# 32x32 transposes in the last step of the modulation, and 128-row operands in the attention scores of two layers

## The chip, the cores and the metric

The kernel runs on one core of a Trainium2 chip. The metric is the device time of one execution in microseconds (us); less is better. The engines of the core have names of their own in the profile: PE is TensorE (matrix products; PEld its loading of weights), DVE VectorE, ACT ScalarE, POOL GpSimd, and SP the queue that issues most of the DMAs.

## The reference, cut to what matters

Two layers over 512 latent tokens and 256 context tokens of width 1024. Each layer takes six vectors (shift, scale and gate for each of two sub-layers) from a conditioning vector, for the latent tokens from `c` and for the context tokens from `c_ctx`. Layer 0 mixes tokens by a recurrence and by windowed attention with a sink, layer 1 by latent attention (`_mla_latent`) and a convolution; each ends in a mixture of experts.

```python
def _modulation(cond, w, b):
    m = (jax.nn.silu(cond) @ w + b)[..., None, :]
    return jnp.split(m, 6, axis=-1)

# layer 0, windowed heads (width 64)
s_win = jnp.einsum('bnqkgd,bnmkd->bnkgqm', qb, kb).astype(jnp.float32) * scale
s_ctx = jnp.einsum('bnqkgd,bckd->bnkgqc', qb, k_ctx).astype(jnp.float32) * scale
s_sink = _sink_column(sink, kvh, g, s_win.shape[:-1] + (1,))
p = jax.nn.softmax(jnp.concatenate([s_win, s_ctx, s_sink], axis=-1), axis=-1)

# layer 1, heads of width 64 + 32
s = jnp.einsum('bqhd,bkhd->bhqk', q, k).astype(jnp.float32) * q.shape[-1] ** -0.5
p = jax.nn.softmax(s, axis=-1).astype(v.dtype)

def reference(...):
    for layer in range(DEPTH):
        m_l = _modulation(c, w_mod[layer], b_mod[layer])
        m_c = _modulation(c_ctx, w_mod[layer], b_mod[layer])
        h_l = _modulate(x_lat, m_l[0], m_l[1])
        ...
        x_lat = _layer_norm(DN_ALPHA * x_lat + m_l[2] * y_l, ...)
        f_l = _modulate(x_lat, m_l[3], m_l[4])
        ffn = _hier_moe(tokens, ...)
        x_lat = _layer_norm(DN_ALPHA * x_lat + m_l[5] * ffn, ...)
```

## The kernel before

Tokens lie along the free axis: 512 latent ones, 4 of padding, 256 of context, W = 772 columns in all. All weights come through one ring of 2 MB buffers that SP fills in the order of their use (`Stream`); a buffer is handed back with `K.stream.done`. The program is written as a sequence of stages (the mixer of layer 0, its routing and experts, the mixer of layer 1, its routing and experts, the output); inside them the order of the instructions on each engine is set by the scheduler of the tile framework, which runs a model of the timeline while it builds (`schedule_with_timeline_sim=True`, line 2273). Each engine then runs its own list in order, and an instruction that waits holds what stands behind it on that engine.

**Modulation.** One section (one of the six vectors of a layer, 1024 wide, for `c` and `c_ctx` together) is computed by `modulation(K, l, sec)` in two halves of 512. `modulation_rows` (line 213) streams a half of the weights through PE as `qmod`: eight products of 32 columns by 512, two to each group of 32 partitions (line 219), so that the four partial sums of a row stand in partitions 0, 32, 64 and 96 for `c` and one below for `c_ctx`. ACT copies `qmod` from PSUM into `msb` (line 222). What is still to be done is to add the four partial sums and to turn the row into columns, since the vectors are used along the partitions. That is `finish()`: 16 products, each with 64 strided columns of `msb` as weights and a 128x2 constant `pick` as the moving operand (line 239), into `fmp`, and one addition on DVE that writes `fm` (line 240). The mixers call this as filling between their own steps: `fill()` runs the `finish()` of the section before and then starts the next. Sections 0 and 1 of layer 0 are done in the beginning by other lines (L364). The other ten go through `modulation`: sections 2 to 5 of layer 0 and sections 0 and 1 of layer 1 in the mixer of layer 0 (line 499), sections 2 to 5 of layer 1 in the attention of layer 1 (line 1987).

**Scores of layer 0.** `maxima(t)` forms a bound of the scores of four heads, as four rows of high and low parts, and turns them by PE into `mT`, a tile of 4 partitions by 768 (lines 583 to 587). `scores` (line 614) adds that bound to the scores inside PSUM by a third product, with `sel`, four rows of a 0/1 constant, as weights and `mT` as moving operand (line 627 for the context's own queries, line 637 for the others). `normalise` uses the same four rows for the sink (line 693).

**Scores of layer 1.** `operands(h, w)` (line 1901) writes, for each head, the high and low parts of queries and keys (`qh`, `ql`, `kh`, `kl`), 96 partitions of values; two more partitions of `kh` hold ones and of `qh` the negative maximum. `mx` (lines 1935 and 1940) are the products for that maximum, `scores` (line 1996) the three products of a block of 128 keys (lines 1999 to 2001), the last of them over 98 partitions. Even heads take their tiles from one pool, odd ones from another, one of each kind.

Of the kernel before, what the change touches and what calls it, by code (L numbers as in the profile page):

```python
# [11 lines left out]
F = mybir.dt.float32  # L12
# [22 lines left out]
def host_arrays(inp):  # L35
# [6 lines left out]
    a["xT"] = x.reshape(NT, 8, 128).transpose(2, 1, 0)  # L42
    a["wmod"] = i["w_mod"].reshape(2, 128, 8, 12, 512).transpose(0, 3, 1, 2, 4).reshape(2, 12, 128, 4096)
    a["lng"], a["lnb"] = i["ln_g"], i["ln_b"]
# [71 lines left out]
    cf["pick"][0::32, 0] = cf["pick"][1::32, 1] = 1  # L116
    cf["eps"] = np.full((128, 1), EPS)
    F_off, o = {}, 0
    for k, v in cf.items():
# [92 lines left out]

def modulation_rows(K, s):

    nc = K.nc
    q = K.ps.tile([128, 512], F, tag="b", name="qmod")
    for k in range(2):
        for c in range(4):
            nc.tensor.matmul(q[32 * c:32 * c + 32], K.cond[:, 2 * c + k, :],  # L219
                             s[0][:, 1024 * c + 512 * k:1024 * c + 512 * k + 512], start=(k == 0), stop=(k == 1))  # L220
    m = K.mp.tile([128, 512], F, tag="msb", name="msb", bufs=2)
    nc.scalar.activation(m, q, AF.Copy)
    return m


def modulation(K, l, sec):

    nc = K.nc
    ms = []
    for b in range(2):  # L230
        s = K.stream.get(("mod", l, sec, b))
        ms.append(modulation_rows(K, s))
        K.stream.done(s)

    def finish():
        t = K.ps.tile([128, 512], F, tag="b", name="fmp")
        for b in range(2):
            for j in range(8):
                nc.tensor.matmul(t[64 * b:64 * b + 64, 2 * j:2 * j + 2], ms[b][:, j::8], K.cst["pick"], start=True, stop=True)
        nc.vector.tensor_tensor(K.fm[:, l, :, sec], t[:, 0:16].rearrange("p (j i) -> p i j", j=8),  # L240
                                K.fmb[:, l, None, sec].to_broadcast([128, 2, 8]), op=ALU.add)

    return finish
# [47 lines left out]
def mixer_even(K):  # L291
# [260 lines left out]
    def maxima(t):  # L552
# [31 lines left out]
        for b in range(6):  # L584
            PE.transpose(q[0:4, 128 * b:128 * b + 128], nb[:, b, :], c["identb"])
        mT = up.tile([4, 768], BF, tag="mT", name="mT", bufs=2)
        V.tensor_copy(mT, q[0:4, 0:768])
        early.append((qs, mT))
# [25 lines left out]
    def scores(h, qs, mT, unit_):  # L614
# [4 lines left out]
        p = ap.tile([128, 512], F, tag="P", name="P", bufs=9)  # L619
        sel = c["sel"][0:4, 128 * par:128 * par + 128]  # L620
        if kind == "x":
# [63 lines left out]
    def normalise(t, mT, ol, oc, sums):  # L685
# [3 lines left out]
        for o, s, n, r0, m0 in ((ol, 0, 512, 0, 0), (oc, 1, 256, C0, 512)):  # L689
            dn, es = ps("dn"), ps("es")  # L690
            for i in range(2):
                PE.matmul(dn[64 * i:64 * i + 64, 0:n], c["onesf"][:, 0:64], sums[i][s][:, 0:n], start=True, stop=True)
            PE.matmul(es[:, 0:n], c["sel"][0:4, 256:384], mT[:, m0:m0 + n], start=True, stop=True)
            e = ap.tile([128, 512], F, tag="es", name="es", bufs=2)
            S.activation(e[:, 0:n], es[:, 0:n], AF.Exp, scale=0.125, bias=sk)
            V.tensor_add(e[:, 0:n], e[:, 0:n], dn[:, 0:n])
            V.reciprocal(e[:, 0:n], e[:, 0:n])
            V.tensor_mul(att[:, r0:r0 + n], o[:, 0:n], e[:, 0:n])
# [969 lines left out]
def mixer_odd(K, uh, hh, hl):  # L1668
# [232 lines left out]
    def operands(h, w):  # L1901
# [11 lines left out]
        V.tensor_add(f[64:96], f[64:96], r[64:96])  # L1913
        pool = ap if h % 2 else op
        qh = pool.tile([98, NL], FR, tag="qh", name="qh")
        ql = pool.tile([96, NL], FR, tag="ql", name="ql")
        S.activation(qh[0:96], f, AF.Copy)
        V.tensor_sub(ql, f, qh[0:96].bitcast(F))
        if h < 2:
            khs[h] = pool.tile([98, W], FR, name="kh%d" % h)  # L1920
        kh = khs[h % 2]
        kl = pool.tile([96, W], FR, tag="kl", name="kl")
        for q, (s0, s1) in zip(kq, both):
# [9 lines left out]
        for b in range(4):  # L1933
            q = ps("mx")
            PE.matmul(q, qh[0:96, 128 * b:128 * b + 128], kh[0:96, 0:NL], start=True, stop=True)
            V.tensor_reduce(mx[:, b, 0:1], q, axis=AX.X, op=ALU.max)
        for b in range(0, 4, 2):
            q = ps("mx")
            for i in range(2):
                PE.matmul(q[:, 256 * i:256 * i + 256], qh[0:96, 128 * (b + i):128 * (b + i) + 128], kh[0:96, C0:W],  # L1940
                          start=True, stop=True)
# [54 lines left out]
    def scores(kh, kl, qh, ql):  # L1996
        for n, tk in enumerate(toks):
            q = ps("s")
            PE.matmul(q, kh[0:96, tk:tk + 128], ql, start=True, stop=False)
            PE.matmul(q, kl[:, tk:tk + 128], qh[0:96], start=False, stop=False)  # L2000
            PE.matmul(q, kh[:, tk:tk + 128], qh, start=False, stop=True)
# [204 lines left out]
def setup(ctx, tc, a, pvo, cfo, cbo):  # L2206
# [20 lines left out]
    def prologue(K):  # L2227
# [8 lines left out]
        K.cst = dict(ident=f("ident"), onesf=f("ones"), iota=f("iota"), iota2=f("iota2"), down=f("down"), tokc=f("tokc"),  # L2236
                     zero=f("zero"), pick=f("pick"), eps=f("eps"), tri=g("tri"), ones=g("ones"), identb=g("ident"), mge=g("mge"),
                     mle=g("mle"), sel=g("sel"))
# [40 lines left out]
```

## Time and profile before

| | us |
|---|---|
| median of 3 runs | 2051.74 |
| lowest, highest | 2051.34, 2056.99 |
| the profiled execution | 2062.3 |
| its span in the trace | 2060.5 |
| PE busy | 1810.0 (88% of the span) |
| PE weight loads | 950.9 (46%) |
| DVE busy | 911.9 (44%) |
| ACT busy | 471.7 (23%) |
| POOL busy | 481.9 (23%) |

The profile is one execution, with times in us from the start of its span. Busy times of PE are lengths of records that overlap, so that the distance between the starts of two neighbours tells better what one costs. A line in it is a line of the kernel before; the changed kernel has its lines 5 to 18 further down. The "granted clock" of PE is given as a share of its upper level, 2.4 GHz; 0.5 is its lower level, 1.2 GHz, and a stretch in between holds both.

### The profile page before, as it was taken

The page shows a single profiled execution, that of the slowest core. Times are in us where ns is not written, and L with a number is a line of the kernel's source. Part 1 is how long each engine was busy: PE and PEld are TensorE (multiplying, and loading weights), DVE is VectorE, ACT ScalarE, POOL GpSimd, SP SyncE. Part 2 cuts the span into 40 slices and gives each one's busy share as a digit, 9 for nine tenths or more (in the row PEclk, how much of TensorE's full clock was granted, in tenths as well). Part 3 has the DMA queues.
Part 4 walks back from the last instruction along what each step waited for, and adds up shares of the span by engine and source line. Part 5 has one row for each costly group of instructions (what it writes and reads, how often), then busy time and mean ns, then how long its engine had stood idle before and what let it go on. Part 6 is the DMA issues. An engine that isn't in the chain of part 4 may idle for free. (4 is left out here: it accounts for less than half of the span.)

```text
span 2060.5 us, 23254 instructions
## 1 busy us (share of the span) xinstructions
PE 1810.0 (88%) x8514; PEld 950.9 (46%) x8515; DVE 911.9 (44%) x1631; ACT 471.7 (23%) x794; POOL 481.9 (23%) x415
## 2 busy tenths in 40 slices
PE   5999999995998989999967787999769999998785
PEld 3668644684333333333335663556633333333232
DVE  3676531577221221222167888465833233322127
ACT  3472322322010110101035453334310000000001
POOL 2142335333000000100033656334100010000103
PEclk9989898996999999999988797889879999999997
DMA  8741320426698999998982112424559999999973
GB/s 350 274 156 42 123 85 1 164 102 256 264 426 371 411 425 424 408 395 349 373 334 92 41 42 110 175 83 187 225 214 423 427 404 400 424 424 425 424 311 150
DMA packets 59023, 551.87 MB, mean 268 GB/s; under 512 B 13295, under 2 KB 13807, under 8 KB 28018
## 3 DMA queue, kind: packets, MB, share of 16 engines
q1 hardware_dynamic: 43490, 514.47, 61.1%
q0 software_dynamic: 11056, 21.00, 2.7%
q10 hardware_dynamic: 4320, 14.31, 1.8%
q8 instruction: 98, 1.61, 0.3%
q14 instruction: 59, 0.48, 0.1%
HBM read 535.00 MB, written 33.61 MB: 276 GB/s over the span
## 5 line engine op out<-in xcount | busy, mean ns | idle before, releaser
L916 PE MATMUL q<-ring,xT 128*64 128x512 f32 x1024 | 475.6, 608 | 43.5 <-PEq L1148 27.9
L917 PE MATMUL q<-ring,xT 128*64 128x512 f32 x1024 | 476.6, 609 | 5.6 <-DMA ring<-in_w_dram 5.6
L945 PE MATMUL q<-ring,hT 128*64 128x512 f32 x1152 | 297.6, 605 | 24.8 <-DMA ring<-in_w_dram 10.9
L916 PEld LDWEIGHTS q<-ring,xT 128*64 128x64 f32 x1024 | 132.3, 139 | 296.4 <-issue 264.6
L925 ACT ACTIVATE sl<-q 64x512 f32<-64x512 f32 x72 | 42.6, 592 | 752.1 <-PE q L917 742.4
L878 POOL DMA_INDIRECT xg<-f,tok x38 | 39.1, 1029 | 591.3 <-DVE tok L873 402.9
L945 PEld LDWEIGHTS q<-ring,hT 128*64 128x64 f32 x1152 | 88.7, 138 | 180.5 <-issue 167.4
L917 PEld LDWEIGHTS q<-ring,xT 128*64 128x64 f32 x1024 | 132.9, 139 | 28.5 <-issue 18.7
L935 DVE COPY hT<-q 128x256 f32<-128x256 f32 x72 | 30.6, 425 | 232.2 <-PE q L933 231.8
L263 PE MATMUL pj<-hh,wlo 128*128 128x512 f32 (+2 forms) x336 | 107.3, 371 | 12.9 <-DVE wlo L252 12.9
L263 PE MATMUL pj<-hl,whi 128*128 128x512 f32 (+2 forms) x336 | 105.0, 364 | 0.0
L263 PE MATMUL pj<-hh,whi 128*128 128x512 f32 (+2 forms) x336 | 104.6, 365 | 0.0
L1815 POOL TENSOR_TENSOR acc<-acc,prod 128x512 f32<-128x512 f32 x56 | 86.5, 1545 | 54.9 <-ACT prod L1814 52.0
L851 DVE TENSOR_TENSOR oh<-cf,pos 128x512 fp32r<-128x512 f32 (+1 forms) x65 | 53.3, 823 | 98.8 <-PE qi L865 97.8
L953 DVE TENSOR_TENSOR y<-q,m 64x512 f32<-64x512 f32 x70 | 48.2, 689 | 83.3 <-PE q L945 75.1
L891 DVE COPY xT<-qx 128x512 f32<-128x512 f32 x32 | 22.1, 692 | 123.2 <-PE qx L887 123.2
L956 DVE COPY y<-q 64x512 f32<-64x512 f32 x37 | 25.7, 693 | 113.9 <-ACT y L955 75.8
L926 DVE SCALAR_TENSOR_TENSOR h<-q,gate,sl 64x512 f32<-64x512 f32 x68 | 51.0, 749 | 56.4 <-ACT sl L925 35.4
L263 PEld LDWEIGHTS pj<-hh,wlo 128*128 128x128 f32 (+1 forms) x336 | 58.4, 195 | 28.9 <-DVE wlo L252 15.1
L1810 DVE SCALAR_TENSOR_TENSOR acc<-glu,pv,acc 128x512 f32<-128x512 f32 x60 | 70.9, 1187 | 0.9
L219 PE MATMUL qmod<-ring,cond 128*32 128x512 f32 x384 | 61.9, 786 | 10.6 <-ACT cond L2241 10.6
L916 PE MATMUL q<-ring,xTo 128*64 128x512 f32 x128 | 61.7, 639 | 8.0 <-DVE xTo L900 8.0
(523 smaller groups left out, 3144.1 us busy)
## 6 DMA issues: line engine op xcount, KB each, us to landing
ring<-in_w_dram SPq DMA_DIRECT2D x192, 2048.0 KB, 18.7
ring<-in_wmod_dram SPq DMA_DIRECT2D x24, 2048.0 KB, 8.7
ring<-Y SPq DMA_DIRECT2D x8, 1024.0 KB, 9.3
ring<-in_ew_dram SPq DMA_DIRECT2D x3, 2048.0 KB, 14.9
f<-t ACTq DMA_DIRECT2D x10, 512.0 KB, 3.3
xhat<-xh ACTq DMA_DIRECT2D x9, 512.0 KB, 3.7
ring<-in_ewo_dram SPq DMA_DIRECT2D x2, 2048.0 KB, 10.1
ring<-in_ow_dram SPq DMA_DIRECT2D x2, 2048.0 KB, 10.2
```

The costliest lines, as they stand in the source:

```text
L219: nc.tensor.matmul(q[32 * c:32 * c + 32], K.cond[:, 2 * c + k, :], s[0][:, 1024 * c + 512 * k:1024 * c + 512 * k + 512], start=(k == 0), s ...
L263: nc.tensor.matmul(q[0:m, 0:s1 - s0], a[:, k, 0:m], b[k][:, s0:s1], start=(k == i == 0), stop=(k == 7 and i == 2))
L851: V.tensor_tensor(oh.rearrange("p t (n s) -> p t n s", n=n), iota[:, None, None, :].to_broadcast([128, T, n, 64]), pos[:, :, e:e + n, None ...
L878: return G.indirect_dma_start(out=x[0:m], out_offset=None, in_=K.f, in_offset=bass.IndirectOffsetOnAxis(ap=tok[0:m], axis=0), bounds_check ...
L916: PE.matmul(q[a:a + 64], xT[:, k, :], w1[:, 512 * k:512 * k + 512], start=(k == 0), stop=(k == 7))
L917: last = PE.matmul(q[b:b + 64], xT[:, k, :], w3[:, 512 * k:512 * k + 512], start=(k == 0), stop=(k == 7)).ins
L925: S.activation(sl[a:a + 64], q[a:a + 64], AF.Silu)
L926: V.scalar_tensor_tensor(h[a:a + 64], q[b:b + 64], gate[a:a + 64], sl[a:a + 64], op0=ALU.mult, op1=ALU.mult)
L945: K.last_mm = PE.matmul(q[64 * o:64 * o + 64], hT[:, k, :], w2[:, 1024 * k + 512 * o:1024 * k + 512 * o + 512], start=(k == 0), stop=(k == ...
L953: V.tensor_mul(y[:, b], q[a], K.m5[a, b])
L1810: V.scalar_tensor_tensor(y, g[:, k:k + NL], w(k), y, op0=ALU.mult, op1=ALU.add)
L1815: G.tensor_add(z, z, p)
```

## The change

It has three parts.

1. `modulation()` no longer copies `qmod` on ACT. DVE transposes it, 32x32 block by 32x32 block, out of PSUM into `msb` (two of 128x512 for each of the ten sections, 20 in all). The weights are laid out on the host in another order of columns, so that each block holds 32 neighbouring elements of the vector. `finish()` then needs 8 products in place of 16, each with a 128x32 constant (`stack`, four unit matrices one below the other) as weights and 8 columns of `msb` as moving operand. The four older sums at line 364 stay as they are.
2. In layer 0 `mT` gets 128 partitions, 124 of them zeroed by POOL, and `sel` is used with all its 128 rows, whose other rows are zero: 64 products in `scores` and 8 in `normalise`.
3. In layer 1 `kh`, `kl`, `qh` and `ql` are tiles of 128 partitions, allocated once for even and once for odd heads; POOL zeroes partitions 96 to 127 of each, and from the third head on it zeroes the two rows of `qh` that held the maximum before. `mx` and `scores` use all 128 partitions.

The diff:

```diff
--- before.py
+++ after.py
@@ -40,7 +40,11 @@
     x = np.concatenate([i["x"][0], i["ctx"][0]], 0)
     a["x"] = x
     a["xT"] = x.reshape(NT, 8, 128).transpose(2, 1, 0)
-    a["wmod"] = i["w_mod"].reshape(2, 128, 8, 12, 512).transpose(0, 3, 1, 2, 4).reshape(2, 12, 128, 4096)
+    wm = i["w_mod"].reshape(2, 128, 8, 12, 512).transpose(0, 3, 1, 2, 4)
+
+    wp = i["w_mod"].reshape(2, 128, 8, 6, 4, 32, 2, 4).transpose(0, 3, 6, 1, 2, 4, 7, 5).reshape(2, 12, 128, 8, 512)
+    first = (np.arange(24).reshape(2, 12) < 4)[:, :, None, None, None]
+    a["wmod"] = np.where(first, wm, wp).reshape(2, 12, 128, 4096)
     a["lng"], a["lnb"] = i["ln_g"], i["ln_b"]
     ew = i["e_w_in"][0].reshape(8, 128, 1792).transpose(1, 0, 2)
     cols = np.concatenate([np.arange(512, 1024), np.arange(1536, 1792), np.arange(1024, 1536), np.arange(0, 512)])
@@ -115,6 +119,7 @@
     cf["pick"] = np.zeros((128, 2))
     cf["pick"][0::32, 0] = cf["pick"][1::32, 1] = 1
     cf["eps"] = np.full((128, 1), EPS)
+    cf["stack"] = np.tile(np.eye(32), (4, 1))
     F_off, o = {}, 0
     for k, v in cf.items():
         F_off[k] = (o, v.shape[1])
@@ -210,7 +215,7 @@
     return K.pv[:, o:o + w]
 
 
-def modulation_rows(K, s):
+def modulation_parts(K, s):
 
     nc = K.nc
     q = K.ps.tile([128, 512], F, tag="b", name="qmod")
@@ -218,8 +223,13 @@
         for c in range(4):
             nc.tensor.matmul(q[32 * c:32 * c + 32], K.cond[:, 2 * c + k, :],
                              s[0][:, 1024 * c + 512 * k:1024 * c + 512 * k + 512], start=(k == 0), stop=(k == 1))
+    return q
+
+
+def modulation_rows(K, s):
+    q = modulation_parts(K, s)
     m = K.mp.tile([128, 512], F, tag="msb", name="msb", bufs=2)
-    nc.scalar.activation(m, q, AF.Copy)
+    K.nc.scalar.activation(m, q, AF.Copy)
     return m
 
 
@@ -229,14 +239,19 @@
     ms = []
     for b in range(2):
         s = K.stream.get(("mod", l, sec, b))
-        ms.append(modulation_rows(K, s))
+        q = modulation_parts(K, s)
         K.stream.done(s)
+
+        m = K.mp.tile([128, 512], F, tag="msb", name="msb", bufs=2)
+        nc.vector.transpose(m, q)
+        ms.append(m.rearrange("p (n y) -> p n y", y=32))
 
     def finish():
         t = K.ps.tile([128, 512], F, tag="b", name="fmp")
         for b in range(2):
-            for j in range(8):
-                nc.tensor.matmul(t[64 * b:64 * b + 64, 2 * j:2 * j + 2], ms[b][:, j::8], K.cst["pick"], start=True, stop=True)
+            for g in range(4):
+                nc.tensor.matmul(t[32 * g:32 * g + 32, 8 * b:8 * b + 8], K.cst["stack"], ms[b][:, 4 * g:4 * g + 4, 0:2],
+                                 start=True, stop=True)
         nc.vector.tensor_tensor(K.fm[:, l, :, sec], t[:, 0:16].rearrange("p (j i) -> p i j", j=8),
                                 K.fmb[:, l, None, sec].to_broadcast([128, 2, 8]), op=ALU.add)
 
@@ -583,8 +598,9 @@
         q = K.ps.tile([128, 1024], BF, tag="b", name="mT")
         for b in range(6):
             PE.transpose(q[0:4, 128 * b:128 * b + 128], nb[:, b, :], c["identb"])
-        mT = up.tile([4, 768], BF, tag="mT", name="mT", bufs=2)
-        V.tensor_copy(mT, q[0:4, 0:768])
+        mT = up.tile([128, 768], BF, tag="mT", name="mT", bufs=2)
+        G.memset(mT, 0.0)
+        V.tensor_copy(mT[0:4], q[0:4, 0:768])
         early.append((qs, mT))
 
     mix, early = [], []
@@ -617,7 +633,7 @@
         q = ps("st")
         kind, j = unit_
         p = ap.tile([128, 512], F, tag="P", name="P", bufs=9)
-        sel = c["sel"][0:4, 128 * par:128 * par + 128]
+        sel = c["sel"][:, 128 * par:128 * par + 128]
         if kind == "x":
             for j in range(2):
                 o = q[:, 256 * j:256 * j + 256]
@@ -690,7 +706,7 @@
             dn, es = ps("dn"), ps("es")
             for i in range(2):
                 PE.matmul(dn[64 * i:64 * i + 64, 0:n], c["onesf"][:, 0:64], sums[i][s][:, 0:n], start=True, stop=True)
-            PE.matmul(es[:, 0:n], c["sel"][0:4, 256:384], mT[:, m0:m0 + n], start=True, stop=True)
+            PE.matmul(es[:, 0:n], c["sel"][:, 256:384], mT[:, m0:m0 + n], start=True, stop=True)
             e = ap.tile([128, 512], F, tag="es", name="es", bufs=2)
             S.activation(e[:, 0:n], es[:, 0:n], AF.Exp, scale=0.125, bias=sk)
             V.tensor_add(e[:, 0:n], e[:, 0:n], dn[:, 0:n])
@@ -1911,15 +1927,17 @@
         V.tensor_mul(f[64:96], qn[64:96], rope[64:96, 0])
         V.tensor_mul(r[64:96], qn[96:128], rope[96:128, 1])
         V.tensor_add(f[64:96], f[64:96], r[64:96])
-        pool = ap if h % 2 else op
-        qh = pool.tile([98, NL], FR, tag="qh", name="qh")
-        ql = pool.tile([96, NL], FR, tag="ql", name="ql")
+        if h < 2:
+
+            pool = ap if h else op
+            khs[h] = [pool.tile([128, n], FR, name="%s%d" % (nm, h)) for nm, n in (("kh", W), ("kl", W), ("qh", NL), ("ql", NL))]
+            for x in khs[h]:
+                G.memset(x[96:128].bitcast(F), 0.0)
+        kh, kl, qh, ql = khs[h % 2]
+        if h > 1:
+            G.memset(qh[96:98].bitcast(F), 0.0)
         S.activation(qh[0:96], f, AF.Copy)
-        V.tensor_sub(ql, f, qh[0:96].bitcast(F))
-        if h < 2:
-            khs[h] = pool.tile([98, W], FR, name="kh%d" % h)
-        kh = khs[h % 2]
-        kl = pool.tile([96, W], FR, tag="kl", name="kl")
+        V.tensor_sub(ql[0:96], f, qh[0:96].bitcast(F))
         for q, (s0, s1) in zip(kq, both):
             src = q[0:64, 0:s1 - s0]
             S.activation(kh[0:64, s0:s1], src, AF.Copy)
@@ -1932,12 +1950,12 @@
         mx = op.tile([128, 4, 2], F, tag="mx", name="mx", bufs=2)
         for b in range(4):
             q = ps("mx")
-            PE.matmul(q, qh[0:96, 128 * b:128 * b + 128], kh[0:96, 0:NL], start=True, stop=True)
+            PE.matmul(q, qh[:, 128 * b:128 * b + 128], kh[:, 0:NL], start=True, stop=True)
             V.tensor_reduce(mx[:, b, 0:1], q, axis=AX.X, op=ALU.max)
         for b in range(0, 4, 2):
             q = ps("mx")
             for i in range(2):
-                PE.matmul(q[:, 256 * i:256 * i + 256], qh[0:96, 128 * (b + i):128 * (b + i) + 128], kh[0:96, C0:W],
+                PE.matmul(q[:, 256 * i:256 * i + 256], qh[:, 128 * (b + i):128 * (b + i) + 128], kh[:, C0:W],
                           start=True, stop=True)
             V.tensor_reduce(mx[:, b:b + 2, 1], q.rearrange("p (i n) -> p i n", i=2), axis=AX.X, op=ALU.max)
         V.tensor_tensor(mx[:, :, 0:1], mx[:, :, 0:1], mx[:, :, 1:2], op=ALU.max)
@@ -1996,8 +2014,8 @@
     def scores(kh, kl, qh, ql):
         for n, tk in enumerate(toks):
             q = ps("s")
-            PE.matmul(q, kh[0:96, tk:tk + 128], ql, start=True, stop=False)
-            PE.matmul(q, kl[:, tk:tk + 128], qh[0:96], start=False, stop=False)
+            PE.matmul(q, kh[:, tk:tk + 128], ql, start=True, stop=False)
+            PE.matmul(q, kl[:, tk:tk + 128], qh, start=False, stop=False)
             PE.matmul(q, kh[:, tk:tk + 128], qh, start=False, stop=True)
             p = ap.tile([128, NL], F, tag="P", name="P", bufs=NP)
             S.activation(p, q, AF.Exp, scale=scale)
```

What the scheduler makes of it: the order of the big steps stays, and the lists differ by the operations that come and go. On PE, in layer 0 behind the third chunk of the projection (`chunk(2)`, `pj`), the rows before are (`fmp` is the finish of a section, `qmod` the products of the next, `gate` the recurrence):

```order
L263 MATMUL pj<-hh,whi 128x512
L263 MATMUL pj<-hh,whi 128x260
L239 MATMUL fmp<-cf,msb 64x2 x16
L219 MATMUL qmod<-ring,cond 32x512 x16
L437 MATMUL gate<-uc,ring 128x512
```

and after:

```order
L278 MATMUL pj<-hh,whi 128x512
L278 MATMUL pj<-hh,whi 128x260
L253 MATMUL fmp<-msb,cf 32x8 x8
L224 MATMUL qmod<-ring,cond 32x512 x16
L452 MATMUL gate<-uc,ring 128x512
```

Sixteen narrow products have become eight, and nothing else has moved. On DVE, at the first `fill()` in layer 0, beside the convolution of the recurrence (`uc`) and the split of the projection's weights (`wlo`), the rows before are:

```order
L421 TENSOR_SCALAR uc<-u,pv 128x772
L423 SCALAR_TENSOR_TENSOR uc<-u,pv,uc 128x772
L252 TENSOR_TENSOR wlo<-ring,whi 128x1024
L423 SCALAR_TENSOR_TENSOR uc<-u,pv,uc 128x772
L252 TENSOR_TENSOR wlo<-ring,whi 128x1024
L421 TENSOR_SCALAR uc<-u,pv 128x772
L423 SCALAR_TENSOR_TENSOR uc<-u,pv,uc 128x772 x4
```

and after:

```order
L436 TENSOR_SCALAR uc<-u,pv 128x772
L246 STREAM_TRANSPOSE msb<-qmod 128x512
L438 SCALAR_TENSOR_TENSOR uc<-u,pv,uc 128x772
L267 TENSOR_TENSOR wlo<-ring,whi 128x1024 x2
L438 SCALAR_TENSOR_TENSOR uc<-u,pv,uc 128x772
L246 STREAM_TRANSPOSE msb<-qmod 128x512
L436 TENSOR_SCALAR uc<-u,pv 128x772
L438 SCALAR_TENSOR_TENSOR uc<-u,pv,uc 128x772 x4
```

The two transposes stand in DVE's list where ACT had its copies before; the first of them, which waits for `qmod`, now stands ahead of the first `wlo`.

## Rows read from the trace of the kernel before

**Rows 1.** Windows by stage: stretch, length, busy us (count) per engine, clock, DMA.

```profile
46.00:230.00 184.00, 181.81 (x1081) 139.96 (x1079) 124.18 (x145) 91.13 (x133) 58.12 (x60) 0.96 0.39 147
230.00:385.00 155.00, 153.20 (x632) 73.60 (x625) 52.06 (x71) 50.19 (x93) 70.25 (x76) 0.87 0.21 82
1230.00:1271.00 41.00, 25.38 (x105) 12.91 (x104) 40.52 (x48) 19.88 (x40) 31.13 (x21) 0.79 0.26 103
1271.00:1420.00 149.00, 142.29 (x703) 85.53 (x703) 84.06 (x138) 53.52 (x101) 51.41 (x43) 0.85 0.27 103
```

**Rows 2.** The sum of the same windows for the tile fmp alone.

```profile
sum 529.00, PE 35.52 PEld 34.78 DVE 1.74; mean PE 8.88 PEld 8.69 DVE 0.43
```

**Rows 3.** Timeline of PE, two finishes: start, length, engine, line, operation, tiles, shapes.

```profile
308.81 3.55 PE L239 MATMUL fmp<-cf,msb 128*64 128x2 f32 x32
...
1275.71 3.55 PE L239 MATMUL fmp<-cf,msb 128*64 128x2 f32 x32
```

**Rows 4.** Windows around finishes; the clock is the third number from the end.

```profile
121.00:128.00 7.00, 7.00 (x41) 2.29 (x40) 4.66 (x6) 6.24 (x9) 3.87 (x10) 0.51 0.04 4
271.00:275.00 4.00, 4.00 (x24) 1.25 (x26) 0.18 (x1) 0.00 (x0) 0.70 (x1) 0.57 0.00 0
309.00:312.00 3.00, 3.00 (x31) 3.00 (x31) 0.00 (x0) 0.52 (x2) 3.00 (x3) 1.00 0.00 0
312.00:333.00 21.00, 21.00 (x50) 8.46 (x49) 0.18 (x1) 3.54 (x7) 8.63 (x16) 0.51 0.00 1
1278.00:1285.00 7.00, 7.00 (x39) 2.56 (x42) 1.25 (x5) 0.60 (x1) 2.20 (x3) 0.52 0.21 43
1329.00:1333.00 4.00, 4.00 (x23) 1.27 (x27) 0.61 (x4) 0.14 (x1) 1.27 (x6) 0.57 0.02 4
```

**Rows 5.** Timeline of PE in layer 1, the nearest narrow products.

```profile
1401.25 1.09 PE L2025 MATMUL rs<-rT,cf 8*64 8x128 f32 x16
```

**Rows 6.** Timeline of PE in layer 0 around a product with sel.

```profile
231.72 0.28 PE L636 MATMUL st<-qs,k 128*128 128x256 f32 x1
231.93 0.28 PE L637 MATMUL st<-mT,cb 4*128 4x256 bf16 x1
232.14 0.23 PE L642 MATMUL st<-cb 128*128 128x128 bf16 x1
...
232.38 0.28 PE L570 MATMUL mw<-k,qs 128*128 128x256 f32 x1
232.50 0.23 PE L574 MATMUL mw<-cb 128*128 128x128 bf16 x1
```

**Rows 7.** Timeline of PE in layer 1, products over 128 and over 96 partitions.

```profile
1258.16 0.40 PE L1895 MATMUL qn<-cqn,wh 128*128 128x512 f32 x1
1258.40 0.40 PE L1896 MATMUL qn<-cqn,wh 128*128 128x512 f32 x1
...
1260.38 0.40 PE L1999 MATMUL s<-ql,kh 96*128 96x512 f32 x1
1260.62 0.40 PE L2000 MATMUL s<-qh,kl 96*128 96x512 f32 x1
```

**Rows 8.** Page, costliest groups: DVE reading a 128x512 tile out of PSUM.

```profile
L891 DVE COPY xT<-qx 128x512 f32<-128x512 f32 x32 | 22.1, 692 | 123.2 <-PE qx L887 123.2
```

**Rows 9.** Tile qmod: who waited for it (us, times), over the whole run.

```profile
  ACT msb L222: 67.9, 19
```

**Rows 10.** Timeline of the first fill in layer 0, with idle time and releaser in brackets.

```profile
59.39 3.63 PE L219 MATMUL qmod<-ring,cond 128*32 128x512 f32 x30
...
60.56 1.02 DVE L423 SCALAR_TENSOR_TENSOR uc<-u,pv,uc 128x772 f32<-128x772 f32 x1
...
61.50 1.22 DVE L252 TENSOR_TENSOR wlo<-ring,whi 128x1024 fp32r<-128x1024 f32 x1
...
62.95 0.30 PEld L263 LDWEIGHTS pj<-hh,wlo 128*128 128x128 f32 x2 [0.84 <-DVE wlo L252]
```

**Rows 11.** POOL's zeroing of two rows in layer 1, by line.

```profile
L1928 POOL MEMSET kh<- x2: 737/858/978, 1198.6 to 1226.9; 2x772 f32 x2
```

More of the change, by code (lines that the diff above doesn't have):

```diff
@@ L2236, in prologue @@
         K.cst = dict(ident=f("ident"), onesf=f("ones"), iota=f("iota"), iota2=f("iota2"), down=f("down"), tokc=f("tokc"),
-                     zero=f("zero"), pick=f("pick"), eps=f("eps"), tri=g("tri"), ones=g("ones"), identb=g("ident"), mge=g("mge"),
+                     zero=f("zero"), pick=f("pick"), eps=f("eps"), stack=f("stack"), tri=g("tri"), ones=g("ones"), identb=g("ident"), mge=g("mge"),
                      mle=g("mle"), sel=g("sel"))
```

## The prediction

> **What bounds the kernel now.** I read the windows by stage first, because the share of busy time on the page is a mean over stages with different limits. The change acts in three of them. In the mixer of layer 0 PE is busy 181.81 of 184 us and 153.20 of 155, in the attention of layer 1 behind 1271 us 142.29 of 149; DVE, ACT and POOL have room there (DVE 124, 52 and 84 us) [rows 1]. What PE saves in these stretches is time. Between 1230 and 1271 it is the other way round: DVE is busy 40.52 of 41 us and PE 25.38, so there a DVE instruction more is time. The transfers don't hold these stages up: their share is 0.21 to 0.39 [rows 1].
>
> The last column but two of the same rows is the second reading: the granted clock is 0.96, 0.87 and 0.85. A stretch of length t at clock c has lost t x (1 - c), at most, against full clock: 184 x 0.04 + 155 x 0.13 + 149 x 0.15 = 7 + 20 + 22 = 50 us. Third, I asked for the tile `fmp`, what runs where the clock falls, and for the neighbours of the products that change.
>
> **Part 1, the finish.** The ten finishes take 35.52 us of PE [rows 2], 3.55 us each in 32 records (16 products, two records each), 111 ns a record [rows 3]. PE does nothing else in that time. The new finish has 8 products, thus 16 records, over a 32-column weight with 8 moving columns. The trace has no such form. Its nearest row is 16 records of 64-column weights with 128 moving columns in 1.09 us, 68 ns each [rows 5]. From below I take half of that, 0.55 us, since the columns of both operands are fewer; from above the old price of a record, 16 x 0.111 = 1.78 us. I take 1.09, the row, as the neighbour in size and count. The saving is 10 x (3.55 - 1.09) = 24.6 us, between 10 x (3.55 - 1.78) = 17.7 and 10 x (3.55 - 0.55) = 30. All of it lies in PE-bound stretches.
>
> The Trainium skill, "TensorE: Matmul & The Clock Gate", section "LDWEIGHTS (loading the stationary operand)", says that loading weights takes as long as their columns divided by 1.2 GHz, whatever the rows. By it 32 columns take 27 ns, and if the load alone set the pace, 160 records would take 4.3 us and the saving would be 31 us; but by it 64 columns would take 53 ns, and the old finish shows 111 [rows 3].
>
> **Part 2, `sel` with 128 rows.** Between products over 128 partitions of 256 columns the starts lie 0.12 us apart (232.38 to 232.50); into the product over 4 partitions they lie 0.21 apart (231.72 to 231.93), and out of it 0.21 again (231.93 to 232.14) [rows 6]. So a change of the number of rows costs about 0.09 us each way. Of the 64 products in `scores`, 48 are followed by another over 128 partitions and 128 columns, and save 0.18; 16 are followed by products with 64-column weights, which stay another form, and save 0.09: 48 x 0.18 + 16 x 0.09 = 10.1 us. The 8 in `normalise` I leave out. The bounds are 0, if the extra belongs to the bf16 product and not to its rows, and 72 x 0.18 = 13. POOL's four zeroings of `mT` have no reader near: POOL is busy 70 of 155 us there [rows 1], and `mT` is needed a whole pair of heads later; if one were late, it would cost what the nearest row of zeroing takes, 0.86 us each [rows 11].
>
> **Part 3, 96 rows to 128 in layer 1.** Products over 96 partitions follow each other at 0.24 us (1260.38 to 1260.62), those over 128 at 0.24 too (1258.16 to 1258.40) [rows 7]. Nothing is gained or lost on PE. The zeroings on POOL (four for each of the first two heads, one for each later head) cost at most 8 x 0.86 + 6 x 0.86 = 12 us of POOL, by the row of a zeroing that is as long and has fewer rows [rows 11]. POOL is busy 31 of 41 and 51 of 149 us [rows 1], so I take 0 and keep, for the first head of each pool, two late ones in the range: 2 us.
>
> **Part 4, the transposes on DVE.** ACT loses 20 copies, DVE gains 20 transposes. No transpose is in the trace; the nearest row is DVE's copy of a 128x512 tile out of PSUM, 0.69 us [rows 8]. 20 x 0.69 = 13.8 us of DVE is the bound from above by load, 0 that from below. Most of it falls where DVE has room. Two places are different. At the first fill in layer 0 the first transpose now stands ahead of the first `wlo`, and PE waits for `wlo` already (0.84 us at 62.95). `qmod` runs from 59.39 for 3.63 us in two halves, so that its first half is there at 61.2; the transpose ends at 61.9, the `uc` that started at 60.56 ends 1.02 later, 62.9, and `wlo` 1.22 later, at 64.1, against 62.72 before [rows 10]: 1.4 us. And in the DVE-bound stretch from 1230 to 1271 two transposes (the section started there) cost 1.4 us, and up to 1 us of waiting for `qmod`: 2.4. Together 4 us.
>
> **Part 5, the clock.** The clock is 1.00 during the finish at 308.81, and from 312 to 333 it is 0.51, though PE is busy without a gap [rows 4]. Five of the falls come with the end of a finish, this one, that at 1275.71 [rows 3] and three others: 121 to 128 (0.51), 271 to 275 (0.57), 312 to 333, 1278 to 1285 (0.52) and 1329 to 1333 (0.57) [rows 4]. In each PE had been at two-column products for some 3 us. They cost 7 x 0.49 + 4 x 0.43 + 21 x 0.49 + 7 x 0.48 + 4 x 0.43 = 3.4 + 1.7 + 10.3 + 3.4 + 1.7 = 20.5 us. With the finish down to about 1 us in a stream of wide products I expect all five to go, and of the other 29 us (50 - 20.5), which fall at stalls and at rows of narrow products elsewhere, a small part, 4 us, since fewer drains keep PE fuller; but new falls may come elsewhere. I take 24.5 us; the bounds are 0 and 50.
>
> **The sum.** 24.6 + 10.1 + 24.5 - 4 = 55 us off the profiled 2062.3, that is 2007. That execution took 10.6 us more than the median of the runs; the same difference from 2051.74 is 1997 us. All terms at their poorest (17.7 + 0 + 0, less 13.8 of DVE and 2 of POOL) give 2050, all at their best (30 + 13 + 50 - 0) 1959; that they all fall on one side I hold for unlikely.
>
> **Rivals.** *The clock doesn't come back.* The falls may belong to something else in the same places (the `qmod` products with 32-column weights come directly behind each finish and stay). For it: not every fall follows a finish, as half of the 50 us shows. Against it: five of ten finishes have one at their end, and the clock is full while they run (309 to 312) [rows 4]. Then the gain is 24.6 + 10.1 - 4 = 31, and the time 2021.
>
> *The rows of `sel` give nothing*, since a product over few rows takes as long as one over 128 and the extra comes from its type. Then 45 us remain: 2007. Against it: the product behind it, which is bf16 too, is late as well, while the bf16 product at 232.50 isn't [rows 6]. The Trainium skill, "TensorE: Matmul & The Clock Gate", section "Why this matters for your kernels", has this rule for a single product over 32 rows; rows 7 agree for 96, rows 6 don't for 4.
>
> *The gain of layer 0 is given back.* If the experts of layer 0 wait for weights, an earlier end of the mixer gains only what the stream of weights moves up too. Of the 55 us some 37 lie in layer 0 (6 of 10 finishes 15, `sel` 10, clock 15, less 3). Against it: the share of the transfers is 0.21 in this stage [rows 1], so the stream stands waiting for buffers that the mixer hands back, and moves with it. Then 18 us remain: 2034.
>
> *Slower.* DVE's list is in order, and a transpose that waits for `qmod` holds what stands behind it. ACT sat 67.9 us in its waits for `qmod`, 19 times over 24 copies [rows 9]; 20 of these on DVE would be 56.6 us, with the transposes' own 13.8 it is 70 us. If all of it reached PE and the clock did not come back, the sum would be 70 - 35 = +35: 2087. It decides from the point where 35 us of it, half, reach PE. Against it: where PE is the bound, DVE idles by 103 and 65 us [rows 1], and a wait for the bound engine's own product is idle time that DVE had anyway.
>
> **How the numbers follow.** Forecast (a gain of 40 us and more, the clock back for most of it) 0.60; clock not back 0.20; `sel` nothing 0.07; given back 0.05; slower 0.06; no difference 0.02. A measurement of this kernel can tell 0.3%, 6 us. Faster by more: 0.60 + 0.20 + 0.07 + 0.05 = 0.92; within 0.02; slower 0.06. The range takes in the first three cases and the bounds of the clock as far as they are likely: from 2051.74 - 82 = 1970 to 2051.74 - 19 = 2033.
>
> **What would show it.** In the profile after, the tile `fmp` should take 11 us of PE in place of 35.5. Neighbours of the products with `sel` should stand 0.12 us apart at 256 columns. The granted clock from 312 to 333 us should be 1.00, and the stages' clocks 0.92 and more. No idle time of PE put down to `msb` or `wlo` should exceed 2 us at the first fill. The forecast is wrong if the stretches behind the finishes stay at 0.5, if PE waits for DVE between 46 and 385 us, or if the experts start earlier and end no earlier.

## The result and the profile after

The changed kernel takes 1994.94 us (median of 4 runs, 1992.5 to 2011.23), the kernel before 2054.36 beside it: a ratio of 0.972 with an interval of 0.9669 to 0.977, so 57 us less (47 to 68; every "us less" below is worked out from such a ratio in the same way). Run once more on another chip (below) it gave 0.9702 (0.9678 to 0.9726). The forecast was 1997, the range 1970 to 2033.

The execution that left the trace took 2011.23 us, the longest of the four; where that lies is told at the end. The stretches that a reader should compare are not equal times but equal work: from the first finish to the sixth, from there to the experts of layer 0, and from the seventh finish to the tenth (the finishes are counted in the order in which they run: six in layer 0, four in layer 1). Windows of the kernel before (columns as in [rows 1]):

```profile
71.55:308.81 237.26, 233.28 (x1265) 157.56 (x1264) 137.35 (x175) 105.48 (x158) 80.27 (x72) 0.93 0.32 123
308.81:509.46 200.65, 177.97 (x806) 120.53 (x805) 111.21 (x212) 55.02 (x94) 86.52 (x71) 0.85 0.32 122
1275.71:1357.21 81.50, 77.72 (x423) 43.79 (x422) 41.24 (x77) 25.12 (x53) 28.17 (x27) 0.85 0.39 155
```

and of the changed kernel:

```profile
71.41:281.51 210.10, 200.07 (x1180) 137.59 (x1183) 145.84 (x185) 100.19 (x149) 82.76 (x74) 0.98 0.35 137
281.51:467.22 185.71, 162.88 (x790) 116.65 (x791) 111.20 (x212) 54.08 (x92) 85.77 (x70) 0.88 0.36 133
1240.53:1306.32 65.79, 60.99 (x376) 31.86 (x375) 46.24 (x84) 21.57 (x46) 26.55 (x28) 0.94 0.49 192
```

They have become 27, 15 and 16 us shorter, PE's busy time by 33, 15 and 17, and the clock rose in each. What PE lost in busy time in the first stretch is not all won: PE now idles 10 us there, before 4.

The finish answers to [rows 3]. Timeline of PE in the changed kernel at the third one:

```profile
110.48 1.46 PE L452 MATMUL gate<-uc,ring 128*128 128x512 f32 x4
111.87 0.31 PE L253 MATMUL fmp<-msb,cf 128*32 128x8 f32 x16
112.02 1.49 PE L224 MATMUL qmod<-ring,cond 128*32 128x512 f32 x12
```

The next product starts 0.15 us after the finish began (111.87 to 112.02), 9 ns a record, where it was 3.48. The ten finishes of this trace take 0.15 to 0.37 us, 2.2 in all.

The product with `sel` answers to [rows 6]. Timeline of PE in layer 0 of the changed kernel:

```profile
282.73 0.28 PE L652 MATMUL st<-qs,k 128*128 128x256 f32 x1
282.85 0.28 PE L653 MATMUL st<-mT,cb 128*128 128x256 bf16 x1
282.97 0.22 PE L658 MATMUL st<-cb 128*128 128x128 bf16 x1
```

It starts 0.12 us after its neighbour, and the next 0.12 after it; both were 0.21.

The clock answers to [rows 4]. Windows of the changed kernel behind the third, the fifth, the sixth and the seventh finish:

```profile
112.00:119.00 7.00, 7.00 (x67) 3.99 (x64) 7.00 (x7) 5.57 (x10) 4.33 (x2) 1.00 0.00 1
246.00:250.00 4.00, 4.00 (x48) 1.30 (x45) 0.89 (x2) 0.00 (x0) 0.00 (x0) 1.00 0.29 66
282.00:303.00 21.00, 20.64 (x93) 9.88 (x96) 7.61 (x8) 7.55 (x16) 15.45 (x23) 1.00 0.00 1
1241.00:1248.00 7.00, 7.00 (x41) 1.56 (x35) 3.42 (x10) 0.24 (x1) 1.44 (x2) 0.79 0.38 122
```

Three of them are at full clock; the 21 us that were at 0.51 behind the sixth are at 1.00. Behind the seventh some of the time is still at the lower level: that fall stands at the end of the stretch in which DVE is the bound. Two more finishes have the lower clock beside them, the fourth (135.50), ahead of which PE had waited for 6.1 us, and the tenth (1306.32), where the fall begins 4 us ahead of the finish:

```profile
134.60:141.50 6.90, 6.00 (x29) 4.79 (x30) 6.87 (x7) 6.89 (x13) 3.26 (x3) 0.51 0.23 89
1302.00:1312.20 10.20, 10.14 (x54) 6.49 (x53) 3.88 (x11) 3.01 (x6) 5.56 (x5) 0.50 0.01 0
```

One more long fall is gone, and it follows no finish. In the kernel before the clock was at its lower level from 233.7 to 250.8 us, among the products with `sel`; in the changed kernel (from 142 to 277 us) and with part 2 alone, which keeps the old finish, there is nothing like it, and with part 1 alone, which keeps the old `sel`, 3.4 us of it:

```profile
233.70:250.80 17.10, 17.06 (x45) 7.60 (x46) 4.08 (x7) 3.65 (x7) 6.51 (x6) 0.50 0.40 170
141.60:276.80 135.20, 132.34 (x779) 93.36 (x781) 80.05 (x120) 42.83 (x68) 50.98 (x41) 1.00 0.25 95
154.50:297.50 143.00, 139.18 (x822) 99.15 (x820) 80.99 (x121) 46.42 (x76) 52.70 (x43) 1.00 0.23 90
222.20:225.60 3.40, 3.40 (x8) 0.83 (x8) 0.87 (x2) 0.96 (x2) 1.81 (x1) 0.51 1.00 429
```

(before, changed, part 2 alone, part 1 alone). What starts that fall was not tested.

The transposes and who waited for them, from the view by tile of `qmod` (their shortest, median and longest in ns; us and times):

```profile
L246 DVE STREAM_TRANSPOSE msb<-qmod x20: 668/707/718, 59.9 to 1286.2; 128x512 f32<-128x512 f32 x20
...
  DVE msb L246: 13.0, 8
```

And what PE waited for from 72 us to the sixth finish, before and after (us in total, times, longest):

```profile
PE fmp L239 <- ACT g L438: 1.9, 1, 1.9
...
PE fmp L253 <- ACT g L453: 6.1, 1, 6.1
```

The fourth finish waits for a PSUM buffer that ACT frees (line 438, now 453, a step of the recurrence). That wait was 1.9 us and is 6.1: PE comes there earlier, the chain of ACT, DVE and POOL that ends in this step does not come earlier by as much. (The chain holds DVE's addition of the third finish, behind whatever stands ahead of it in DVE's list.)

### The profile page after: what moved, and what is told of

It is laid out like the page before. It is cut to its first block, busy times and chain, and to the rows that moved or that the text cites. A ratio compares the mean times of both kernels' runs of the same rounds, so it can differ in the third digit from the quotient of the medians.

```text
span 2009.5 us, 22936 instructions
## 1 busy us (share of the span) xinstructions
PE 1743.5 (87%) x8347; PEld 910.7 (45%) x8355; DVE 935.1 (47%) x1651; ACT 459.3 (23%) x774; POOL 493.8 (25%) x433
## 5 line engine op out<-in xcount | busy, mean ns | idle before, releaser
L941 ACT ACTIVATE sl<-q 64x512 f32<-64x512 f32 x72 | 42.6, 592 | 756.5 <-PE q L933 745.3
L972 DVE COPY y<-q 64x512 f32<-64x512 f32 x37 | 25.7, 693 | 112.5 <-ACT y L971 74.5
L976 POOL DMA_INDIRECT Y<-y,idx x33 | 32.8, 993 | 148.2 <-DVEq L1164 73.2
```

Of the source, the lines that this page charges most:

```text
L941: S.activation(sl[a:a + 64], q[a:a + 64], AF.Silu)
L976: st = G.indirect_dma_start(out=Y.rearrange("r (n d) -> (r n) d", n=n), out_offset=bass.IndirectOffsetOnAxis(ap=idx[r], axis=0), in_=y[r], ...
```

## The experiments

**The parts apart.** Three kernels, each with one part of the change: `e1_finish` has the hunks of the modulation (transposes, layout of the weights, `stack`), `e2_sel` those of `mT` and `sel`, `e3_rows` those of layer 1. They are the hunks of the diff above.

> Part 1 alone (transposes on DVE and the new finish), layers' scores as before. Theory: the finish falls from 3.48 us (start to the next product) to 0.15 to 0.4 as in the changed kernel, 33 us for ten, the clock behind the finishes comes back for some 20, and DVE's transposes cost 5 to 10: 43 to 48 us less than before, about 2007. Rival (the clock's return belongs to the scores): 33 - 8 = 25 us less, about 2028, and the stretch behind the finish at some 309 us is at 0.5 as before. Rival (the transposes cost nothing and the finish brings all): 55 us or more.

> Part 2 alone (sel and mT with 128 rows in layer 0). Theory: 48 x 0.18 + 16 x 0.09 = 10 us less than before, 2043, the neighbours at 256 columns 0.12 us apart in place of 0.21, the clock behind the finishes still 0.5. Rival (the clock in layer 0 hangs on these products): 10 + some 15 = 25 us less, 2028. Rival (rows give nothing): 2053.

> Part 3 alone (128 rows in layer 1). Theory: PE's products stay 0.23 us apart, the zeroings on POOL fall beside DVE's work in the stretch where DVE is the bound: 0 to 5 us more than before, 2053 to 2058. Rival (the higher rows raise the clock in layer 1): 5 to 10 us less.

Measured: part 1 alone 2007.3 us, ratio 0.977 (0.9745 to 0.9794), 47 us less; part 2 alone 2032.84, 0.9907 (0.9882 to 0.9932), 19 us less; part 3 alone 2053.11, 0.999 (0.9976 to 1.0004), no difference. The first theory held, the third too. Part 2 is worth more than its 10 us of PE, near to its rival. The three sum to 68 us, the whole change is worth 57 to 61. The intervals alone would allow that difference; the traces show that something is counted twice, and that it is the clock. Lengths of the three stretches, and in brackets what the lower clock cost in them at most (length times one minus the clock):

| us | before | part 1 alone | part 2 alone | changed |
|---|---|---|---|---|
| first to sixth finish | 237.3 (16.6) | 216.0 (4.3) | 226.9 (11.3) | 210.1 (4.2) |
| sixth finish to experts | 200.7 (30.1) | 186.9 (18.7) | 187.5 (20.6) | 185.7 (22.3) |
| seventh to tenth finish | 81.5 (12.2) | 67.9 (8.1) | 81.6 (12.2) | 65.8 (3.9) |
| sum | 519.4 (58.9) | 470.8 (31.1) | 496.0 (44.1) | 461.6 (30.4) |

The two parts gain 48.6 and 23.4 us here, 72, and the change 57.8: 14 less than their sum. Of the clock they gain 27.8 and 14.8, 42.6, and the change 28.5: 14 less too. Windows of part 2 alone (with the old finish), behind the sixth finish at 296.69:

```profile
297.00:305.00 8.00, 8.00 (x45) 5.69 (x45) 0.17 (x1) 1.47 (x3) 4.82 (x11) 0.57 0.00 0
305.00:320.00 15.00, 14.97 (x69) 7.07 (x69) 4.29 (x4) 5.21 (x11) 8.07 (x10) 1.00 0.00 1
```

and of part 1 alone (with the old `sel`), behind its sixth finish at 286.68:

```profile
286.00:310.00 24.00, 24.00 (x116) 10.29 (x114) 7.63 (x8) 9.24 (x18) 16.96 (x24) 1.00 0.00 1
```

With the old finish the clock still falls, but with the full-height products behind it comes back within some 8 us and not after 21; with the new finish it does not fall at all here, whichever products stand behind. So in the mixer of layer 0 the two parts share one gain.

**Is it the finish that lowers the clock?** Two twins of the changed kernel, each with some 3.4 us more of PE work in every finish, that nobody reads: `e5_narrow` adds the sixteen old products behind the new ones, `e6_wide` four products of 128x128 by 512 ahead of them.

```diff
 e5_narrow
+        for b in range(2):
+            for j in range(8):
+                nc.tensor.matmul(t[64 * b:64 * b + 64, 16 + 2 * j:18 + 2 * j], raw[b][:, j::8], K.cst["pick"], start=True, stop=True)
 e6_wide
+        for j in range(4):
+            nc.tensor.matmul(t, K.cst["ident"], raw[j % 2], start=True, stop=True)
```

> The changed kernel with the sixteen old products (64-column weights, two moving columns) added behind each new finish; nobody reads their results. That is some 3.4 us of PE for each of ten. Theory (the clock falls by what PE does in these 3.4 us): the changed kernel's 1995 + 34 + 15 to 25 for the clock, 2044 to 2054, with stretches at 0.5 behind several finishes, and 5 us or more above the twin with wide products. Rival (the clock's falls have nothing to do with the finishes): 2029, like the twin.

> The twin: the changed kernel with four products of 128 rows by 128 columns by 512 moving columns (f32) added ahead of each new finish, about 8 records of 0.43 us, 3.4 us of PE; nobody reads their results. Theory: 1995 + 34 = 2029 and no stretch at 0.5 behind a finish that the changed kernel doesn't have. Rival: the same as the narrow twin, within 5 us, whatever that is.

Measured: narrow 2039.26, 0.992 (0.9886 to 0.9953); wide 2027.86, 0.9856 (0.9814 to 0.9899), 11 us apart with intervals that just overlap; the narrow twin lies 5 us below the range that was expected. The traces tell them apart. Windows of the narrow twin, behind its six finishes in layer 0, and over all from the first to the sixth:

```profile
75.00:79.00 4.00, 4.00 (x24) 0.97 (x21) 3.37 (x5) 0.00 (x0) 0.00 (x0) 0.59 0.64 182
96.00:103.00 7.00, 7.00 (x46) 2.99 (x48) 7.00 (x9) 0.00 (x0) 2.73 (x1) 0.52 0.19 37
126.00:131.00 5.00, 5.00 (x34) 1.83 (x37) 4.29 (x7) 4.22 (x5) 2.24 (x8) 0.66 0.02 1
150.00:155.00 5.00, 5.00 (x24) 4.52 (x25) 3.45 (x4) 4.98 (x7) 4.49 (x3) 0.66 0.48 195
263.00:271.00 8.00, 8.00 (x48) 2.99 (x46) 0.89 (x2) 0.00 (x0) 0.48 (x1) 0.57 0.24 59
304.00:308.00 4.00, 4.00 (x18) 2.79 (x17) 0.17 (x1) 0.98 (x2) 2.16 (x10) 0.57 0.00 0
72.00:300.00 228.00, 222.90 (x1319) 154.86 (x1318) 144.25 (x185) 99.28 (x148) 81.86 (x73) 0.95 0.32 124
```

and of the wide twin, in the same places:

```profile
75.00:79.00 4.00, 4.00 (x44) 1.32 (x46) 3.42 (x5) 0.00 (x0) 0.00 (x0) 1.00 0.75 309
96.00:103.00 7.00, 7.00 (x58) 2.60 (x57) 7.00 (x8) 0.79 (x1) 3.58 (x1) 1.00 0.39 117
...
72.00:300.00 228.00, 222.31 (x1267) 146.69 (x1267) 146.26 (x186) 101.62 (x152) 88.81 (x84) 1.00 0.33 128
```

PE is busy for the same 222 us of 228. Behind each of six finishes with narrow products the clock falls; with wide ones of the same length it is 1.00 throughout. By equal work, from the first finish to the sixth, the narrow twin takes 229.7 us and the wide one 220.8: 9 us, of which the clock explains up to 228 x 0.05 = 11. From the seventh to the tenth it is 82.8 and 79.2. The theory holds: what PE did in those 3.4 us lowers the clock, not that they were there. Which old finish is followed by a fall differs from trace to trace, though: in the trace of the kernel before the first two are not, in that of part 2 alone the fifth is not. And whether the few moving columns, the many loads of weights or something else about the narrow products does it, the twins don't separate.

**Why is the new finish so cheap?** It has fewer products, 32-column weights, eight moving columns and neighbours in different column groups of the array, all at once. `e4_pairs` is the kernel before with its two loops exchanged, and nothing else: neighbours alternate between columns 0 to 63 and 64 to 127.

```diff
-        for b in range(2):
-            for j in range(8):
+        for j in range(8):
+            for b in range(2):
                 nc.tensor.matmul(t[64 * b:64 * b + 64, 2 * j:2 * j + 2], ms[b][:, j::8], K.cst["pick"], start=True, stop=True)
```

> The kernel before with the two loops of the finish exchanged, so that neighbouring products go to different halves of the array (columns 0 to 63, then 64 to 127); same count, same shapes, no transposes. Theory (the 111 ns a record come from eight products in a row that load weights into the same half): 55 ns a record or less, the finish 1.8 us or less in place of 3.48, 17 us or more from ten, and some of the clock behind them: 20 to 40 us less than before. Rival (the price goes by record): 3.48 us as before, and 2053.

Measured: 2037.33 us, 0.9909 (0.9888 to 0.9929), 19 us less than before for two exchanged lines. Timeline of PE at its first finish:

```profile
72.01 2.09 PE L239 MATMUL fmp<-cf,msb 128*64 128x2 f32 x32
74.03 1.06 PE L219 MATMUL qmod<-ring,cond 128*32 128x512 f32 x8
```

The same 32 records take 2.02 us (72.01 to 74.03), 63 ns each in place of 109 (3.48 / 32). So the order alone, with the same products, was 1.46 of the 3.48 us: the theory, though a little less than it said (55 ns a record, 20 us or more).

`e8_quads` goes on: no transposes, the copies stay on ACT as before, 32 products of 32-column weights and two moving columns, in turn over four column groups; part 2 as in the change, part 3 as before.

```diff
+        for j in range(8):
+            for g in range(4):
+                o = 256 * (g % 2) + j
+                nc.tensor.matmul(t[32 * g:32 * g + 32, 2 * j:2 * j + 2], ms[g // 2][:, o:o + 249:8], K.cst["pick"],
+                                 start=True, stop=True)
```

> No transposes: the copies stay on ACT, the finish has 32 products with 32-column weights and two moving columns, in an order in which neighbours go to the four column groups in turn; part 2 as in the changed kernel, part 3 as before. Theory (turns of column groups make the finish cheap, not the transposed layout, and the transposes cost 5 us in the DVE-bound stretch and 1 to 5 in layer 0): 64 records of 10 to 31 ns, 0.65 to 2 us a finish; the stretch to the first finish of layer 1 back at 175 us; 1985 to 2005. Rival (the finish is cheap for its 8 moving columns and its fixed weights): 64 x 63 = 4 us a finish, about 2035.

Beside it ran `e7_no_rows`, the change without part 3:

> The changed kernel without its part 3 (layer 1 with 96 and 98 rows as before). Theory: part 3 is worth nothing, 1990 to 1997, and the 5 us that the stretch from the first projection of layer 1 to its first finish has lost stay lost, since they belong to the transposes. Rival (the zeroings on POOL cost them): 1988 or less, with that stretch back at 175 us.

Measured: `e8_quads` 2003.18, 0.9744 (0.9713 to 0.9774); `e7_no_rows` 1998.27, 0.9726 (0.9697 to 0.9756). They can't be told apart, nor from the change; part 3 is worth nothing here either. Timeline of PE at the third finish of `e8_quads`:

```profile
111.65 1.17 PE L240 MATMUL fmp<-cf,msb 128*32 128x2 f32 x64
112.66 0.62 PE L219 MATMUL qmod<-ring,cond 128*32 128x512 f32 x4
```

64 records in 1.01 us, 16 ns each, with two moving columns and other weights in every product. So the finish gets most of its speed without the transposes, by the order and the narrower weights (from 63 to 16 ns both the width of the weights and the number of column groups in turn have changed, and no run separates them); the transposed layout then brings 16 records in place of 64, 0.15 to 0.37 us in place of 1.0 to 1.1, some 8 us for ten, and DVE pays for it. What that costs is looked for between the starts of the finishes, in PE's rows of each trace:

| us | before | changed | `e7_no_rows` | `e8_quads` |
|---|---|---|---|---|
| first projection to first finish | 39.6 | 42.0 | 41.0 | 40.2 |
| third to fourth finish | 25.7 | 23.6 | 23.6 | 21.9 |
| first projection of layer 1 to seventh finish | 174.8 | 180.4 | 180.0 | 175.8 |

With the transposes the first row is 41.0 to 42.0 us in the changed kernel, `e7_no_rows` and part 1 alone (41.5); without them 39.6 to 40.3 in the kernel before, `e8_quads` and parts 2 and 3 alone. The second row is 1.7 us longer with the transposes although its finish is 0.86 shorter. From the first finish to the fourth `e7_no_rows` takes 63.79 us and `e8_quads` 63.82: three finishes that are shorter by 0.86 each win nothing there, and PE's wait at the fourth is longer by just their 2.6 us (6.1 and 3.5). The wait's chain holds DVE's addition of the third finish, at 120.21 and 117.01 us, and DVE is busy almost without a gap in the 35 us ahead of it, more so with the transposes:

```profile
85.50:120.20 34.70, 34.70 (x224) 22.68 (x223) 34.50 (x33) 28.14 (x39) 13.35 (x14) 1.00 0.39 155
...
82.50:117.00 34.50, 34.50 (x309) 22.64 (x308) 32.98 (x31) 29.84 (x42) 13.82 (x14) 1.00 0.41 165
```

(`e7_no_rows`, then `e8_quads`). Two transposes, 1.4 us, lie in that stretch; that all of the 2.6 us is theirs is not shown. The third row holds no finish: 4 to 5 us more with the transposes. But the next stretch turns the balance. From the seventh finish to the tenth `e7_no_rows` takes 65.2 us and `e8_quads` 73.8:

```profile
1232.92:1298.10 65.18, 61.89 (x376) 32.65 (x375) 43.83 (x81) 21.52 (x46) 26.91 (x26) 0.92 0.50 194
...
1232.14:1305.91 73.77, 70.34 (x520) 38.54 (x519) 41.55 (x76) 25.19 (x52) 27.70 (x27) 0.85 0.44 172
```

Of these 8.6 us the three finishes are 2.6, and the clock is up to 73.8 x 0.15 - 65.2 x 0.08 = 5.9. From the first projection of layer 1 to the tenth finish the kernel without transposes is thus 4.4 us slower. Why its clock is lower there is not shown.

**A mixture.** `e9_mixed` is `e7_no_rows` with the finish of `e8_quads` and no transposes for the three sections whose transposes fall into these three rows; beside it, on the same chip, the changed kernel once more.

```diff
+PLAIN = ((0, 2), (0, 5), (1, 2))
+        if (l, sec) in PLAIN:
+            ms.append(modulation_rows(K, s))
```

> The changed kernel without part 3, and with the finish of 32 products in turn (no transposes, copies on ACT, about 1.0 us) for the three sections whose transposes lay on the path: 2 and 5 of layer 0 and 2 of layer 1. Theory: the transposes' 1.3 us ahead of the second finish's chunk, 2.6 between the third and the fourth finish and 2.7 in the DVE-bound stretch come back, three finishes cost 0.86 more each: 6.6 - 2.6 = 4 us less than the changed kernel in the same batch. Rival (the waits move to the next late chain): no difference.

> The changed kernel once more, beside the mixed one on the same chip: 1995 to 2000, a ratio of 0.970 to 0.975. Every theory expects the same of it.

Measured: 1996.82, 0.9704 (0.9683 to 0.9726), and 1995.75, 0.9702 (0.9678 to 0.9726): no difference, the rival. In its trace the first row above is 39.7, a gain, but PE's wait at the fourth finish is still there, and the third row is 177.8, half way. Waits of PE from 46 to 300 us in `e9_mixed`, and in `e8_quads`, which has no transpose at all:

```profile
PE fmp L261 <- ACT g L465: 5.4, 1, 5.4
...
PE fmp L240 <- ACT g L440: 3.5, 1, 3.5
```

The wait grows as the three finishes ahead of it get shorter: 1.9 us with 3.5 each, 2.4 with 2.0 (`e4_pairs`), 3.5 with 1.0, 5.4 in this mixture with one of 1.0 and two of 0.15, 6.1 with 0.15. The twins, with all transposes and 3.7 us in each finish, have 1.9 again (`e6_wide`, then `e5_narrow`):

```profile
PE fmp L253 <- ACT g L456: 1.9, 1, 1.9
...
PE fmp L254 <- ACT g L457: 1.9, 1, 1.9
```

So the transposes alone don't lengthen it: PE comes there earlier than the chain can follow. Taking the transposes of one section away gained nothing there. No version beat the change by more than can be measured.

## Why the prediction was right, step by step

- **Part 1, the finish: right in kind, mis-sized.** The saving was put at 24.6 us between 17.7 and 30; by the starts in PE's rows it is 34.8 - 2.2 = 32.6, outside. The step that failed is the choice of the row for the new form: 68 ns a record from [rows 5], where 9 to 23 were measured. That row had narrow products too, but nothing in it says whether its neighbours lie in different column groups; `e4_pairs` (109 to 63 ns by the order alone) shows that this is part of the price, and `e8_quads` (16 ns) how far it falls with narrower weights as well. What the Trainium skill, "TensorE: Matmul & The Clock Gate", section "LDWEIGHTS (loading the stationary operand)", gives for the load of 32 columns (27 ns, columns by 1.2 GHz) would have made the saving 31 us, as an estimate. The trace agrees neither with that load nor with a pace set by it: here the loads take 106 to 158 ns each, and the 16 of the third finish lie within 0.22 us, so they run side by side.

```profile
111.87 0.22 PEld L253 LDWEIGHTS fmp<-msb,cf 128*32 128x32 f32 x16 [0.34 <-ACT g L453]
...
L253 PEld LDWEIGHTS fmp<-msb,cf x160: 106/112/158, 71.4 to 1306.5; 128*32 128x32 f32 x160
```

- **Part 2, `sel`: right.** 0.21 us became 0.12 on both sides, and the gain of part 2 alone in the three stretches without the clock is 23.4 - 14.8 = 8.6 us, near the 10.1 of the sum. Not foreseen: that its rows also act on the clock (part 2 alone, 19 us in all).
- **Part 3: right.** 0.999, and with or without it the change takes the same.
- **Part 4, the transposes: too low.** 4 us foreseen; the rows above give about 1.5 (foreseen 1.4), 2.6 that shorter finishes don't win ahead of the fourth (foreseen 0, and not all shown to be the transposes') and 4 to 5 (foreseen 2.4), some 9. The price of one was right (0.69 foreseen, 0.707 measured). What was left out is the fourth finish: the row of PE's waits showed 1.9 us there already, and the working did not ask what is late next once PE is earlier. The sign "if PE waits for DVE" has thus half come: PE waits for ACT, behind a chain that goes through DVE.
- **Part 5, the clock: right in size, in part by luck.** 24.5 us foreseen, 20.5 of them behind finishes and 4 elsewhere. In the three stretches it lost 237.26 x 0.07 + 200.65 x 0.15 + 81.50 x 0.15 = 59 us before and 210.10 x 0.02 + 185.71 x 0.12 + 65.79 x 0.06 = 30 after, 29 us less. The five falls at the end of a finish became one of 7 us at 0.79, 19 us less, and that the finishes lower the clock is shown by the twins. But 17.1 x 0.50 = 8.5 us more are the one fall from 233.7 to 250.8, which follows no finish; it is gone with part 2 alone and down to 3.4 us with part 1 alone, so its cause is not separated. One sign failed: from 1236 to 1385 us, in the attention of layer 1, the clock is 0.89, where 0.92 and more was expected.
- **The sum.** 32.6 + 10 + 29 - 9 = 63, where 55 was foreseen and 57 (47 to 68) and 61 were measured; the clock's 29 is a bound from above, since at the lower clock PE also waited. Part 1 was 8 us too low, part 5 some 4, and part 4 5 us too low on the other side; that the forecast came out within 2 us of the median is in part luck.
- **The rivals.** *The clock doesn't come back*: fell with the windows behind the finishes. *`sel` gives nothing*: fell with 0.12 us. *The gain is given back*: the experts of layer 0 last 530 us before and 532 after, so they start 42 us earlier and end 40 earlier. *Slower*: the transposes waited 13.0 us for `qmod`, 8 times, and not the 56.6 of the rival.

## What to carry to other kernels

A row of tiny products is not priced by its count alone but also by which columns of the array its neighbours use (109 and 63 ns a record here): before a layout is changed for it, exchange the loops so that neighbours take turns. A few microseconds of narrow products can cost as much again behind them, if the clock falls (10 us behind the sixth finish, which took 3.5); read the granted clock right behind such rows. And when an engine becomes faster, its small waits of today are the place to look for what is late tomorrow.

## What was not expected of the hardware

Two executions of the same program, on two chips, lie 22 us apart, and what the clock can cost differs by nearly as much. Span and mean granted clock of the changed kernel, in the first profile and in the one of `e10_changed`:

```profile
core 0: 2009.5 us, clock 0.929
```

```profile
core 0: 1987.8 us, clock 0.939
```

2009.5 x 0.071 = 143 us and 1987.8 x 0.061 = 121 us are lost, at most, against full clock: a difference of 21 of the 22 us. From the tenth finish to the end, where no part of the change acts, the two take 703.1 and 690.1 us. So a single profile of this kernel is not good for differences below 1%, and the stretches that a change touches are to be compared one by one.
